# Two groups of tiny loads added to GpSimd's queue in a batched matmul-trace kernel

## The chip, the cores and the metric

The kernel runs on one core of a Trainium2 chip. The time is device time in microseconds (us) of one execution on that core. Before the change it was 707.68 us, the median of 3 runs (707.53 to 707.79).

The core has a matrix engine (TensorE, PE in the profile), a vector engine (VectorE, DVE), a scalar engine (ScalarE, ACT), a general engine (GpSimd, POOL) and a synchronizing engine (SyncE, SP). 16 DMA engines move data between the main memory (HBM) and the on-chip memory (SBUF). An engine starts a transfer by an issue on its own queue, and the transfer counts up a semaphore, by 16 in all, when it has landed.

## The reference

```python
def setup_inputs():
    B, N = 8, 2176
    return {"a": np.random.randn(B, N, N).astype(np.float32),
            "b": np.random.randn(B, N, N).astype(np.float32)}

def reference(a, b):
    prod = np.matmul(a, b)
    return np.diagonal(prod, axis1=1, axis2=2).sum(axis=-1).astype(np.float32)
```

For each of 8 batches it is the trace of A times B. The kernel never forms the product: the trace is the sum over all i and k of A[i,k] * B[k,i], so it transposes A and takes the sum of the elementwise product of A's transpose with B.

## The kernel before

A batch is two matrices of 2176 by 2176 float32 numbers, some 19 MB each, and every one of them is read once. The loads convert to bfloat16 on the way, which is why nearly all of them stand on GpSimd's queue. A matrix comes in two transfers: `middle` (5 of its 17 blocks of 128 rows) and a side tile (the other 12 blocks, as 2 groups of 6 rows for each partition). The tiles are `a_side`, `b_side`, `middle` (used by A first and then by B) and `at`, the transpose of A. There is one of each.

For a batch, PE transposes A block by block into three PSUM tiles (`fill0` to `fill2`, L301 to L311), and ACT and DVE copy these to `at` (`evacuate`, L212): of four fills, DVE takes one. Then DVE multiplies `at` by B and sums, by one instruction for the part in `middle` and one for the part in `b_side` (`rows_product`, L239, by the instruction at L234), each into a column of `sums`. A matrix product with a column of ones adds up the partitions at the end.

The order of the loads is written out by hand in GpSimd's program (L149 to L202), with waits on semaphores between them. For each batch: the middle of A (L152 or L158; from the second batch on it waits for the first product of the batch before, L157), the side of A (L162, behind a wait for the transposes of the batch before, L161), the middle of B (L176, when PE has read A's middle, L175), and the side of B (L184, when DVE has taken the second product of the batch before, L180). For the first batch a fifth of A's middle is loaded by ACT (L135) without conversion, and ACT and DVE convert it.

In the last batch the side of B comes in pieces, so that little work is left when the last byte has landed: first 6 blocks at once (L189), then three pieces by `LATE_SLICES` (L194 to L198: 3 blocks, 1 and 1), then three parts of the last block by `LAST_PIECES` (L199 to L202), each with a semaphore of its own. PE multiplies most of these (L347), DVE the rest. Small PE products that nobody reads keep PE busy between the pieces.

After its last load GpSimd counts up a semaphore 16 times (L203), drains (L207: it waits until its own work is done), waits for the last product (L208) and clears the kernel's semaphores (L209). SP stores the result (L144), and GpSimd's wait for that store (L358) ends the program.

The queue of GpSimd is in order: what is issued later is carried out later by each DMA engine. So a load that is issued early waits behind those already in the queue, and while something is queued the DMA engines have work.

Of the kernel before, what the change touches and what calls it, by code (L numbers as in the profile page):

```python
# [10 lines left out]
def kernel(  # L11
# [6 lines left out]
    nc = tc.nc  # L18
    P = 128
# [7 lines left out]
    f32 = mybir.dt.float32  # L27
# [16 lines left out]
    sb = ctx.enter_context(tc.tile_pool(name="sb", bufs=1))  # L44
# [10 lines left out]
    sums = sb.tile([P, 2 * (BATCH - 1)], f32, tag="sums")  # L55
    late_acc = sb.tile([P, NT], f32, tag="late")
    result = sb.tile([P, BATCH], f32, tag="result")

    fill_tiles = [ps.tile([P, 8, P], f32, tag=f"fill{j}", name=f"fill{j}") for j in range(BUFS)]
    trace_ps = ps.tile([P, P], f32, tag="trace")  # L60
# [2 lines left out]
    sem = {}  # L63

    own = ["first", "a_mid", "a_all", "b_mid", "b_all"]
    own += [f"piece{k}" for k in range(len(LATE_SLICES) + len(LAST_PIECES))]
    own += ["cleared", "constant", "cast", "mid_in", "all_in", "filled", "at_done", "early"]
    own += [f"free{j}" for j in range(BUFS)]
    for name in own:
        sem[name] = nc.alloc_semaphore(name)  # L70
    numbers = sorted(sem[name].num for name in own)
# [4 lines left out]
    def group(src, start, g, m):  # L76

        rows = src[start:start + P * g * m, :]
        return rows.rearrange("(g p r) k -> p g (r k)", g=g, r=m)
# [49 lines left out]
    plain = b_side.bitcast(f32).rearrange("p r k -> p (r k)")[:, :N]  # L129
    half = N // 2  # L130

    with tc.tile_critical(no_gpsimd_drain=True):

        first = a[0, 0:MID * P, :].rearrange("(p r) k -> p r k", r=MID)
        nc.scalar.dma_start(out=plain, in_=first[:, MID - 1, :]).then_inc(sem["first"], 16)  # L135
        for bi in range(BATCH):
# [8 lines left out]
            out=out.rearrange("(a b) -> a b", a=1), in_=result[:1, :BATCH],  # L145
# [3 lines left out]
        for bi in range(BATCH):  # L149
            last = bi == BATCH - 1  # L150
            if bi == 0:
                nc.gpsimd.dma_start(  # L152
                    out=middle[:, 0:MID - 1, :].rearrange("p r k -> p (r k)"),
                    in_=first[:, 0:MID - 1, :].rearrange("p r k -> p (r k)"),
                ).then_inc(sem["a_mid"], 16)
            else:
                nc.gpsimd.wait_ge(sem["product"], 2 * bi - 1)  # L157
                nc.gpsimd.dma_start(  # L158
                    out=middle.rearrange("p (g r) k -> p g (r k)", g=1), in_=group(a[bi], 0, 1, MID),
                ).then_inc(sem["a_mid"], 16)  # L160
                nc.gpsimd.wait_ge(sem["filled"], per_batch * bi)  # L161
            nc.gpsimd.dma_start(  # L162
                out=a_side.rearrange("p (g r) k -> p g (r k)", g=2),
                in_=group(a[bi], MID * P, 2, SIDE),
            ).then_inc(sem["a_all"], 16)
            if bi == 0:
                for t in (identity32, identity16):
                    nc.gpsimd.memset(t, 0.0).then_inc(sem["cleared"], 1)
                for k, t in enumerate((identity32, identity16)):
                    nc.gpsimd.wait_ge(sem["cleared"], 2)  # L170
                    nc.gpsimd.affine_select(
                        out=t, in_=t, compare_op=mybir.AluOpType.not_equal, fill=1.0, base=0,
                        pattern=[[-1, P]], channel_multiplier=1,
                    ).then_inc(sem["constant"], 1)
            nc.gpsimd.wait_ge(sem["filled"], per_batch * bi + mid_fills)  # L175
            nc.gpsimd.dma_start(  # L176
                out=middle.rearrange("p (g r) k -> p g (r k)", g=1), in_=group(b[bi], 0, 1, MID),
            ).then_inc(sem["b_mid"], 16)
            if bi:
                nc.gpsimd.wait_ge(sem["product"], 2 * bi)  # L180
            else:
                nc.gpsimd.wait_ge(sem["cast"], 2)
            if not last:
                nc.gpsimd.dma_start(  # L184
                    out=b_side.rearrange("p (g r) k -> p g (r k)", g=2),
                    in_=group(b[bi], MID * P, 2, SIDE),
                ).then_inc(sem["b_all"], 16)
                continue
            nc.gpsimd.dma_start(  # L189
                out=b_side[:, 0:SIDE, :].rearrange("p (g r) k -> p g (r k)", g=1),  # L190
                in_=group(b[bi], MID * P, 1, SIDE),
            ).then_inc(sem["b_all"], 16)
            rows = b[bi, LAST * P:N, :].rearrange("(p r) k -> p r k", r=SIDE)
            for k, (r, m) in enumerate(LATE_SLICES):  # L194
                nc.gpsimd.dma_start(  # L195
                    out=b_side[:, SIDE + r:SIDE + r + m, :].rearrange("p r k -> p (r k)"),
                    in_=rows[:, r:r + m, :].rearrange("p r k -> p (r k)"),
                ).then_inc(sem[f"piece{k}"], 16)  # L198
            for k, (lo, mid, hi) in enumerate(LAST_PIECES):  # L199
                nc.gpsimd.dma_start(  # L200
                    out=b_side[:, MOST - 1, lo:hi], in_=rows[:, SIDE - 1, lo:hi],
                ).then_inc(sem[f"piece{len(LATE_SLICES) + k}"], 16)  # L202
# [2 lines left out]
        stored = nc.gpsimd.alloc_register("stored")  # L205
        nc.gpsimd.reg_mov(stored, 16)
        nc.gpsimd.drain()  # L207
        nc.gpsimd.wait_ge(sem["product"], 2 * (BATCH - 1) + 1)  # L208
        nc.gpsimd.sem_clear(range(numbers[0], numbers[-1] + 1))  # L209

# [12 lines left out]
        for _ in range(20):  # L223
# [3 lines left out]
            out=middle[:, MID - 1, :half], in_=plain[:, :half]  # L227
# [11 lines left out]
        def rows_product(v0, rows, acc):  # L239
# [10 lines left out]
            out=middle[:, MID - 1, half:], in_=plain[:, half:]  # L250
        ).then_inc(sem["cast"], 1)
        for bi in range(BATCH):
# [12 lines left out]
            out=result[:1, 0:BATCH - 1],  # L265
            in_=total[:, 0:2 * (BATCH - 1)].rearrange("o (b n) -> o b n", n=2),
# [17 lines left out]
        for k, (lo, mid, hi) in enumerate(LAST_PIECES):  # L284
# [8 lines left out]
            out=result[:1, BATCH - 1:BATCH], in_=total[:, early:early + cols],  # L293
# [96 lines left out]
```

## Time and profile before

| | |
|---|---|
| median of 3 runs | 707.68 us (707.53 to 707.79) |
| the profiled execution | 707.76 us |
| its span, first to last instruction | 706.0 us |
| DVE busy | 380.1 us, 54% |
| PE busy | 209.0 us, 30% |
| ACT busy | 202.5 us, 29% |
| GpSimd busy | 24.5 us, 3% |
| GpSimd's DMA queue (q0) | 7392 packets, 150.96 MB written, 99.7% of the 16 engines' span |
| all DMA packets | 7544, of them 626 under 512 B |
| HBM read | 303.04 MB, 429 GB/s over the span |
| side of A or B: issue to landing, median | 54.7 us and 52.1 us |
| middle of A or B: issue to landing, median | 24.5 us and 22.0 us |

The profile counts the bytes that are written: 2 for each number loaded with conversion, where 4 are read. A transfer is cut into packets, each of them carried by one of the 16 engines. "Busy" is the time in which an engine had at least one instruction in work. The 40 slices of the page are 17.65 us each.

### The profile page before, as it was taken

The page shows a single profiled execution, that of the slowest core. Times are in us where ns is not written, and L with a number is a line of the kernel's source. Part 1 is how long each engine was busy: PE and PEld are TensorE (multiplying, and loading weights), DVE is VectorE, ACT ScalarE, POOL GpSimd, SP SyncE. Part 2 cuts the span into 40 slices and gives each one's busy share as a digit, 9 for nine tenths or more (in the row PEclk, how much of TensorE's full clock was granted, in tenths as well). Part 3 has the DMA queues.
Part 4 walks back from the last instruction along what each step waited for, and adds up shares of the span by engine and source line. Part 5 has one row for each costly group of instructions (what it writes and reads, how often), then busy time and mean ns, then how long its engine had stood idle before and what let it go on. Part 6 is the DMA issues. An engine that isn't in the chain of part 4 may idle for free. (4 is left out here: it accounts for less than half of the span.)

```text
span 706.0 us, 3981 instructions
## 1 busy us (share of the span) xinstructions
PE 209.0 (30%) x1641; PEld 190.6 (27%) x1643; DVE 380.1 (54%) x96; ACT 202.5 (29%) x158; POOL 24.5 (3%) x46
## 2 busy tenths in 40 slices
PE   0335003450134501244013440125401353012547
PEld 0335002440124401244013430124301243012535
DVE  0105488154871539716396163961639616395268
ACT  1427002370024700246003450044500455004540
POOL 1000000000000000000000000000000000002000
PEclk9859555695556955669556785556855677556778
DMA  9999999999999999999999999999999999999997
GB/s 231 219 212 209 228 211 215 216 225 213 221 220 213 206 224 216 215 213 227 209 224 221 211 210 226 214 215 219 221 207 225 222 207 214 224 217 215 225 205 156
DMA packets 7544, 152.14 MB, mean 216 GB/s; under 512 B 626, under 2 KB 882, under 8 KB 1266
## 3 DMA queue, kind: packets, MB, share of 16 engines
q0 software_dynamic: 7392, 150.96, 99.7%
q10 hardware_dynamic: 144, 1.11, 0.4%
q8 instruction: 2, 0.03, 0.0%
q14 instruction: 4, 0.03, 0.0%
q1 hardware_dynamic: 2, 0.00, 0.0%
HBM read 303.04 MB, written 0.00 MB: 429 GB/s over the span
## 5 line engine op out<-in xcount | busy, mean ns | idle before, releaser
L220 ACT COPY at<-fill 128x1536 bf16<-128x1536 bf16 (+3 forms) x156 | 200.1, 1371 | 472.1 <-DVE sums L234 356.5
L234 DVE CUSTOM_DVE_ANT_0 at<-at,b_side 128x26112 bf16<-128x26112 bf16 (+4 forms) x11 | 202.9, 18459 | 83.5 <-DMA b_side<-in_b_dram 83.5
L220 DVE COPY at<-fill 128x1536 bf16<-128x1536 bf16 (+2 forms) x52 | 83.9, 1614 | 221.2 <-PE fill L310 220.8
L310 PE MATMUL fill<-identity,middle 128*128 128x128 f32 (+1 forms) x440 | 69.9, 346 | 370.6 <-PEq L308 370.6
L310 PEld LDWEIGHTS fill<-identity,middle 128*128 128x128 f32 (+1 forms) x440 | 64.8, 182 | 375.3 <-issue 374.9
L310 PE MATMUL fill<-identity,a_side 128*128 128x128 f32 (+1 forms) x1056 | 124.6, 278 | 112.2 <-PEq L308 111.7
L310 PEld LDWEIGHTS fill<-identity,a_side 128*128 128x128 f32 (+1 forms) x1056 | 114.8, 167 | 122.2 <-issue 121.8
L234 DVE CUSTOM_DVE_ANT_0 at<-at,middle 128x10880 bf16<-128x10880 bf16 x8 | 91.9, 11490 | 11.0 <-ACTq L221 11.0
L176 POOL DMA_DIRECT2D middle<-in_b_dram x8 | 4.5, 563 | 335.2 <-PE fill L310 335.2
L158 POOL DMA_DIRECT2D middle<-in_a_dram x7 | 3.9, 563 | 292.1 <-DVE sums L234 292.1
L347 PE MATMUL trace_ps<-b_side,at 128*128 128x128 bf16 x122 | 10.0, 251 | 9.4 <-DMA b_side<-in_b_dram 9.3
L347 PEld LDWEIGHTS trace_ps<-b_side,at 128*128 128x128 bf16 x122 | 9.1, 116 | 11.3 <-DMA b_side<-in_b_dram 10.7
L162 POOL DMA_DIRECT2D a_side<-in_a_dram x8 | 5.7, 714 | 0.0
L184 POOL DMA_DIRECT2D b_side<-in_b_dram x7 | 5.0, 713 | 0.0
L347 PE MATMUL fill<-at 128*128 128x512 bf16 x19 | 4.8, 379 | 0.1
L249 DVE CAST middle<-b_side 128x1088 bf16<-128x1088 f32 x1 | 0.7, 726 | 4.9 <-DMA b_side<-in_a_dram 4.9
L347 PEld LDWEIGHTS fill<-at 128*128 128x128 bf16 x21 | 1.9, 98 | 1.5
L226 ACT ACT_TABLE_LOAD x1 | 1.3, 1283 | 2.7 <-issue 2.7
L226 ACT CAST middle<-b_side 128x1088 bf16<-128x1088 f32 x1 | 1.1, 1098 | 2.0 <-DMA b_side<-in_a_dram 2.0
L200 POOL DMA_DIRECT2D b_side<-in_b_dram x3 | 1.6, 587 | 0.0
L195 POOL DMA_DIRECT2D b_side<-in_b_dram x3 | 1.6, 558 | 0.0
L234 DVE DVE_READ_ACCUMULATOR2_ANT sums<- 128x1 f32 x14 | 1.2, 83 | 0.0
(17 smaller groups left out, 4.2 us busy)
## 6 DMA issues: line engine op xcount, KB each, us to landing
a_side<-in_a_dram POOLq DMA_DIRECT2D x8, 6528.0 KB, 54.7
b_side<-in_b_dram POOLq DMA_DIRECT2D x7, 6528.0 KB, 52.1
middle<-in_b_dram POOLq DMA_DIRECT2D x8, 2720.0 KB, 22.0
middle<-in_a_dram POOLq DMA_DIRECT2D x7, 2720.0 KB, 24.5
b_side<-in_b_dram POOLq DMA_DIRECT2D x1, 3264.0 KB, 37.5
middle<-in_a_dram POOLq DMA_DIRECT2D x1, 2176.0 KB, 14.7
b_side<-in_b_dram POOLq DMA_DIRECT2D x1, 1632.0 KB, 44.9
b_side<-in_a_dram ACTq DMA_DIRECT2D x1, 1088.0 KB, 5.1
```

The source lines that it names most:

```text
L158: nc.gpsimd.dma_start(out=middle.rearrange("p (g r) k -> p g (r k)", g=1), in_=group(a[bi], 0, 1, MID),).then_inc(sem["a_mid"], 16)
L162: nc.gpsimd.dma_start(out=a_side.rearrange("p (g r) k -> p g (r k)", g=2), in_=group(a[bi], MID * P, 2, SIDE),).then_inc(sem["a_all"], 16)
L176: nc.gpsimd.dma_start(out=middle.rearrange("p (g r) k -> p g (r k)", g=1), in_=group(b[bi], 0, 1, MID),).then_inc(sem["b_mid"], 16)
L184: nc.gpsimd.dma_start(out=b_side.rearrange("p (g r) k -> p g (r k)", g=2), in_=group(b[bi], MID * P, 2, SIDE),).then_inc(sem["b_all"], 16)
L195: nc.gpsimd.dma_start(out=b_side[:, SIDE + r:SIDE + r + m, :].rearrange("p r k -> p (r k)"), in_=rows[:, r:r + m, :].rearrange("p r k -> p ...
L200: nc.gpsimd.dma_start(out=b_side[:, MOST - 1, lo:hi], in_=rows[:, SIDE - 1, lo:hi],).then_inc(sem[f"piece{len(LATE_SLICES) + k}"], 16)
L220: copy(out=dst, in_=src).then_inc(sem[f"free{i % BUFS}"], 1)
L226: nc.scalar.copy(out=middle[:, MID - 1, :half], in_=plain[:, :half]).then_inc(sem["cast"], 1)
L234: return nc.vector.tensor_tensor_reduce(out=x if out is None else out, in0=x, in1=y, scale=1.0, scalar=0.0, op0=MUL, op1=ADD, accum_out=acc,)
L249: nc.vector.tensor_copy(out=middle[:, MID - 1, half:], in_=plain[:, half:]).then_inc(sem["cast"], 1)
L310: done = nc.tensor.transpose(into, block, identity)
L347: done = nc.tensor.matmul(trace_ps if real else fill_tiles[0][:, 0:4, :], x, y, start=(n == 0 or not real), stop=(n == len(work) - 1 or no ...
```

## The change

A tile `marks` of 2560 words on each partition is added, with a semaphore of its own. A helper `mark(base)` issues 19 loads from A's first matrix into it on GpSimd's queue, without conversion. The first 15 load 1 to 15 partitions (n partitions of base + n words each). Then a GpSimd instruction resets a cursor of the software that spreads transfers over the DMA engines (`reset_dge_cursor`). The last four load 4 partitions in 4 segments each, of base/2 + 1 to base/2 + 4 words. Nothing reads `marks`.

`mark(16)` stands behind the first batch's load of B's side (L184 of before), ahead of the wait for the first product. `mark(32)` stands in the last batch behind the first of the `LATE_SLICES` loads, ahead of the five last pieces. Behind the drain at the end, GpSimd also waits until the 38 loads have landed (38 x 16 = 608 counts), and the range of semaphores that it clears is longer by one.

```diff
+    marks = sb.tile([P, 2560], f32, tag="marks")
...
+    own += ["marks"]
...
+    marked, at_word = 0, 0
+
+    def mark(base):
+
+        nonlocal marked, at_word
+        for n in range(1, 16):
+            nc.gpsimd.dma_start(
+                out=marks[0:n, at_word:at_word + base + n], in_=a[0, 0:n, 0:base + n],
+            ).then_inc(sem["marks"], 16)
+            marked += 16
+            at_word += base + n
+        nc.gpsimd.inc_swdge_sem([], [], mode="reset_dge_cursor")
+        for n in range(1, 5):
+            nc.gpsimd.dma_start(
+                out=marks[0:4, at_word:at_word + 4 * (base + 16)].rearrange(
+                    "p (g w) -> p g w", g=4)[:, :, 0:base // 2 + n],
+                in_=a[0, 0:4, 0:256].rearrange("p (g w) -> p g w", g=4)[:, :, 0:base // 2 + n],
+            ).then_inc(sem["marks"], 16)
+            marked += 16
+            at_word += 4 * (base + 16)
...
                     in_=group(b[bi], MID * P, 2, SIDE),
                 ).then_inc(sem["b_all"], 16)
+                if bi == 0:
+                    mark(16)
                 continue
...
                 ).then_inc(sem[f"piece{k}"], 16)
+                if k == 0:
+                    mark(32)
             for k, (lo, mid, hi) in enumerate(LAST_PIECES):
...
         nc.gpsimd.drain()
+        nc.gpsimd.wait_ge(sem["marks"], marked)
         nc.gpsimd.wait_ge(sem["product"], 2 * (BATCH - 1) + 1)
```

## The prediction

> **What bounds the kernel now.** I read the slices and queues of the page first, then the chain of work that ended last, then GpSimd's timeline, then the list of DMA issues.
>
> ```profile
> DMA  9999999999999999999999999999999999999997
> GB/s 231 219 212 209 228 211 215 216 225 213 221 220 213 206 224 216 215 213 227 209 224 221 211 210 226 214 215 219 221 207 225 222 207 214 224 217 215 225 205 156
> DMA packets 7544, 152.14 MB, mean 216 GB/s; under 512 B 626, under 2 KB 882, under 8 KB 1266
> ## 3 DMA queue, kind: packets, MB, share of 16 engines
> q0 software_dynamic: 7392, 150.96, 99.7%
> ```
>
> The 16 DMA engines are busy in every slice but the last, and GpSimd's queue q0 takes 99.7% of them. Nothing else is near that: DVE, the busiest engine, has 54%. So whatever lengthens the stream of packets lengthens the kernel, wherever in the stream it stands. The end agrees:
>
> ```profile
> 649.61 0.52 POOL b_side L189
> 650.13 44.91 DMA b_side<-in_b_dram
> 695.04 0.05 issue
> ...
> 701.58 0.39 another core or an unknown queue
> ...
> 702.53 0.09 another core or an unknown queue
> 702.61 0.05 issue
> 702.66 0.65 PE trace_ps L347 x6
> ```
>
> (start, length, what). PE waits for one piece after another as it lands; from the last landing, 702.97 in the trace's semaphore records, to the end at 706.0 everything is a fixed sequence. DVE too ends on the pieces: in the timeline it idles 0.17 us for the fourth before 701.99. So the end moves with the last landing.
>
> ```profile
> 25.18 0.72 POOL L184 DMA_DIRECT2D b_side<-in_b_dram  x1
> 79.67 0.57 POOL L158 DMA_DIRECT2D middle<-in_a_dram  x1 [53.77 <-DVE sums L234]
> ...
> 649.61 0.54 POOL L189 DMA_DIRECT2D b_side<-in_b_dram  x1
> 650.13 1.61 POOL L195 DMA_DIRECT2D b_side<-in_b_dram  x3
> 651.69 1.64 POOL L200 DMA_DIRECT2D b_side<-in_b_dram  x3
> ```
>
> GpSimd issues far ahead of the engines: it idles 53.77 us behind the place of the first group, and the pieces behind the second group are issued some 45 us before they land.
>
> **The change part by part.**
>
> Issue time. 19 loads at the spacing of the last issues (1.61 us for three, some 0.52 us each) are 9.9 us per group. Group one ends near 36, long before 79.67, where GpSimd waits for the first product anyway; it would cost from 53.77/19 = 2.8 us a load. Group two moves the issue of five pieces from 650.7 to about 660.6. The first engine is done with the piece ahead near 693.4, and the longest time from an issue to a first packet in the trace is 3.6 us (1.45 to 5.05), so it costs only above (693.4 - 3.6 - 650.7)/19 = 2.1 us a load. I take nothing for both; the rows of 0.52 to 0.72 us are far below. The cursor reset is one GpSimd instruction of the kind that took 27 ns at the program's start: nothing, behind the same cover.
>
> Packets. This is the term that counts, and the packet records of the trace price it. A completion packet (4 bytes) took 22 ns and a 512 byte packet 60 ns, but they overlap. From the completion packets of the last pieces on the first engine, one piece took 2608, 1705, 651 and 349 ns, with 8 packets of 4352, 2816, 1024 and 512 bytes written. At 0.0735 ns a byte (26112 bytes took 1942 ns, 512 took 60) the bytes are 2560, 1656, 602 and 301 ns. What remains is 48 ns each time: 8 packets and one completion. A whole batch, 48 packets, four completions and 1,183,744 bytes an engine, comes round every 87.294 us, of which the bytes are 87.040: 254 ns remain. The two equations give 3.8 ns a packet and 17.6 ns a completion.
>
> For loads without a cast the ACT queue shows 8704 bytes in 328 ns, 0.0368 ns a byte. Each group has 19 completions on every engine (before: 608 packets of 4 bytes for 38 loads, 16 each). Rows and segments: 120 + 64 = 184 packets in group one; in group two 194, since the listing of instructions shows its first row cut into 11 parts of 3 words. That is 11.5 and 12.1 an engine, with 15.3 and 25.1 KB in all.
> - Group one: 19 x 17.6 + 11.5 x 3.8 + 35 = 413 ns.
> - Group two: 19 x 17.6 + 12.1 x 3.8 + 58 = 438 ns.
> - Sum 0.85 us, all on the path, as the engines never wait.
>
> Bounds: if a completion costs no more than any packet, 61.6 x 3.8 + 93 = 0.33 us. If all 48 ns of a piece were its completion's and a tiny packet cost as much as a 512 byte one in its row (41.5 ns), 38 x 48 + 23.6 x 41.5 = 2.8 us. Below nothing is excluded: no byte is taken away. I take 0.85, since two rows fix it. It lies near the lower end because a tiny load is almost all completion and completions overlap.
>
> How the packets spread matters little: at even shares an engine has 11.5. Were all loads to start on the same engine, that one would carry 15 + 16 = 31 and pay 19.5 x (3.8 + 3) = 0.13 us more a group. The trace of before has only loads of 128 partitions and cannot show it. The Trainium skill (DMA: Bandwidth & Descriptors, "Why a DMA increments its semaphore by 16 and not by 1") says that GpSimd's loads on fewer engines take consecutive ones from a round-robin cursor, and that all 16 post the completion. By it the rows of 1 to 15 fill every engine 7 or 8 times and the four segmented loads once each: the even sum, where the other reading would add 0.26 us.
>
> Drain and wait. GpSimd's drain at L207 gets 38 more loads to wait out, all landed before the last pieces; the new wait for their count follows it and is fulfilled by then. Behind it stand the clearing of semaphores and the wait for the output's landing. I take nothing, with a doubt that is the second rival.
>
> Forecast: the profiled execution took 707.76 us (its span of 706.0 and 1.76 around it) and would take 708.61; the median of the runs is 0.08 lower, 707.68, and 707.68 + 0.85 = **708.5**, its own range 708.0 to 709.0. That is 0.12% more, and 0.2% (1.4 us) is about what a measurement of this kernel can tell from no change.
>
> **The rivals.**
>
> 1. *Tiny packets cost more than the two equations say* (709.1 to 710.5). No row has a data packet under 512 bytes in this queue, and if a read's latency is not covered for some 31 tiny packets in a row, the price goes to the upper bound. For it: nothing in before tests it. Against: the 512 byte packets lost nothing beyond their bytes.
>
> 2. *The drain walks its list* (slower). In the instruction records L207's drain ends at 704.56, 1.59 us after the last landing, far more than a drain without loads behind it (34 to 187 ns). If that is a walk over 38 loads, it is 42 ns each, and 76 loads make it 3.18 us. GpSimd's wait for the output ended at 705.18 and it was ready for it near 704.84, so 0.33 us are covered; from 8 added loads on the drain decides the end. Price 1.59 - 0.33 = 1.26 us, time 709.8. Against: loads that landed long before could have been ticked off while it waited.
>
> 3. *Each tiny load holds its engine until it has landed.* The last completion packet ended at 702.70 and counted at 702.97: 0.27 us, times 38 is 10.3 us, 718. Against: the last three pieces landed at 701.97, 702.61 and 702.97 with 48 ns beyond their bytes. The Trainium skill (same page, "Anatomy of one DMA — SWDGE (gpsimd) path") speaks against the change more strongly: about 2.0 us fixed per DMA, mostly completion. Paid 38 times in a row that would be an estimated 76 us; by those landings the trace does not agree that it is paid in a row.
>
> 4. *Nothing is seen* (707.4 to 708.0): the last engine's final completion counts 0.26 us behind the next one's and 1.45 behind the first one's, and that engine might be spared most of the packets. 5. *Faster*: only if the uneven engines were evened out; no row gives a way.
>
> **How the numbers follow.** Forecast 0.40; tiny packets dearer 0.18 (0.02 of it still within 0.2%); drain 0.28; engine held, or issue beyond its cover, 0.06; nothing 0.05; faster 0.03. Within 0.2%: 0.40 + 0.02 + 0.05 = 0.47. Slower: 0.16 + 0.28 + 0.06 = 0.50. Faster: 0.03. The forecast is the likeliest single case, though the slower ones together hold slightly more. The range 708.0 to 710.6 takes in the forecast, both ends of the packet price and the drain on top of it, and leaves out 0.14.
>
> **What would show it.** Packets rise from 7544 by 38 x 16 + 184 + 194 = 986 to about 8530, nearly all under 512 B; fewer mean that not all engines post completions. The issues of `marks` last near 0.5 us each; the wait before the next batch's middle load shrinks from 53.77 by some 10 us and its start stays near 79.7. The last landing moves from 702.97 to about 703.8 and the drain still ends 1.6 us behind it; near 3.2 it is rival 2. Landings later than 704.4 mean rival 1, and issues above 2 us each would make the forecast wrong from GpSimd's side.

## The result, and the profile after

The changed kernel takes 713.31 us (median of 3 runs, 712.88 to 713.52) against 707.68 us: 5.63 us more, ratio 1.0079 with a 95% interval of 1.0056 to 1.0102. It is slower, by less than one per cent but clear of the noise, and by more than the range allowed for. The profiled execution took 713.31 us, its span is 711.2 us.

Queue and packets, from the page of the changed kernel:

```profile
GB/s 234 213 215 221 213 183 230 210 215 226 208 216 220 215 216 222 211 220 219 212 225 213 216 221 210 227 213 214 223 208 224 220 205 226 210 217 226 211 213 118
DMA packets 8760, 152.19 MB, mean 214 GB/s; under 512 B 1842, under 2 KB 2098, under 8 KB 2482
q0 software_dynamic: 8608, 151.01, 99.7%
```

The queue is as full as before by its share of time, but the sixth slice (88.9 to 106.7 us) moved 183 GB/s where before it was 211. That is where group one stands, behind the first batch's side of B. 1216 packets came on top, not 986. By their sizes they are 608 completions, 250 rows, 32 segmented partitions (one packet each, the segments joined) and 326 fillers of 4 or 16 bytes. That is 32 packets for each load, so by these counts an engine without a share in a load carries a filler, and each load put two packets on every engine.

A closer look at that place: three stretches of the kernel before, and then the same three of the changed kernel (busy time of the engines, clock, and as the last two columns the DMA engines' share and GB/s):

```profile
89.00:91.00 2.00, 0.00 (x0) 0.00 (x0) 0.00 (x0) 0.00 (x0) 0.00 (x0) 0.50 0.83 176
91.00:95.00 4.00, 0.00 (x0) 0.00 (x0) 3.55 (x1) 0.00 (x0) 0.00 (x0) 0.50 1.09 234
95.00:105.00 10.00, 0.41 (x2) 0.44 (x3) 10.00 (x1) 0.00 (x0) 0.00 (x0) 0.50 1.04 223
```

```profile
89.00:91.00 2.00, 0.00 (x0) 0.00 (x0) 0.00 (x0) 0.00 (x0) 0.00 (x0) 0.50 1.83 185
91.00:95.00 4.00, 0.00 (x0) 0.00 (x0) 3.39 (x1) 0.00 (x0) 0.00 (x0) 0.50 0.46 93
95.00:105.00 10.00, 0.00 (x0) 0.00 (x0) 10.00 (x1) 0.00 (x0) 0.00 (x0) 0.50 1.03 222
```

A packet's time is put down where it starts, so a share can be over 1. In the changed kernel 15 engines have started a packet of the next load by 90.8 and the last one by 91.6, and none starts another before 93.5: 1.83 and then 0.46. The packet records show why: 16 packets of 21,760 bytes just behind the group took 3.26 to 3.67 us, where the median is 1.62. The list of DMA issues shows what they stood behind (KB, and us from issue to landing):

```profile
marks<-in_a_dram POOLq DMA_DIRECT2D x1, 0.1 KB, 65.0
marks<-in_a_dram POOLq DMA_DIRECT2D x1, 0.1 KB, 64.7
marks<-in_a_dram POOLq DMA_DIRECT2D x1, 0.2 KB, 64.4
marks<-in_a_dram POOLq DMA_DIRECT2D x1, 0.3 KB, 64.1
```

They were issued some 0.5 us apart and each stayed 0.3 us less in the queue than the one ahead, so they landed some 0.2 us apart, 19 of them in about 4 us, though the packets of one engine start and end within some 0.3 us.

GpSimd's side is as forecast:

```profile
25.78 7.43 POOL L140 DMA_DIRECT2D marks<-in_a_dram  x15
33.20 2.39 POOL L147 DMA_DIRECT2D marks<-in_a_dram  x4
79.01 0.57 POOL L181 DMA_DIRECT2D middle<-in_a_dram  x1 [43.42 <-DVE sums L262]
...
654.32 7.41 POOL L140 DMA_DIRECT2D marks<-in_a_dram  x15
661.72 2.38 POOL L147 DMA_DIRECT2D marks<-in_a_dram  x4
```

0.5 us a load, the wait 10.35 us shorter and ended no later. The end of the chain (start, length, what):

```profile
665.72 40.75 DMA b_side<-in_b_dram
...
706.52 0.65 PE trace_ps L375 x6
...
707.78 0.15 DVE result L320
```

The last piece lands at 706.82, 3.86 us later than before. The end moved by 5.23 us, from 705.99 to 711.22, so 1.37 us more were lost behind the last landing. There GpSimd's drain ends at 709.98, 3.16 us after the landing; it was 1.60 us. The drain before, and then that of the changed kernel (its length in ns, given three times as there is only one, and its start):

```profile
L207 POOLq DRAIN  x1: 50866/50866/50866, 653.7 to 653.7; - x1
```

```profile
L234 POOLq DRAIN  x1: 43876/43876/43876, 666.1 to 666.1; - x1
```

Two costs, then: 1.93 us for each group in the stream, and 1.4 us at the end.

### The profile page after: what moved, and what is told of

Read it like the earlier page. It is cut to its first block, busy times and chain, and to the rows that moved or that the text cites. A ratio compares the mean times of both kernels' runs of the same rounds, so it can differ in the third digit from the quotient of the medians.

```text
span 711.2 us, 4022 instructions
## 1 busy us (share of the span) xinstructions
PE 208.6 (29%) x1641; PEld 189.4 (27%) x1643; DVE 380.3 (53%) x96; ACT 202.3 (28%) x158; POOL 44.0 (6%) x84
## 5 line engine op out<-in xcount | busy, mean ns | idle before, releaser
L140 POOL DMA_DIRECT2D marks<-in_a_dram x30 | 14.8, 506 | 0.0
L207 POOL DMA_DIRECT2D b_side<-in_b_dram x7 | 4.9, 706 | 0.0
L147 POOL DMA_DIRECT2D marks<-in_a_dram x8 | 4.8, 601 | 0.0
L220 POOL DMA_DIRECT2D b_side<-in_b_dram x3 | 1.7, 568 | 0.0
```

Source lines behind the costliest of these rows:

```text
L140: nc.gpsimd.dma_start(out=marks[0:n, at_word:at_word + base + n], in_=a[0, 0:n, 0:base + n],).then_inc(sem["marks"], 16)
L147: nc.gpsimd.dma_start(out=marks[0:4, at_word:at_word + 4 * (base + 16)].rearrange("p (g w) -> p g w", g=4)[:, :, 0:base // 2 + n], in_=a[0 ...
L207: nc.gpsimd.dma_start(out=b_side.rearrange("p (g r) k -> p g (r k)", g=2), in_=group(b[bi], MID * P, 2, SIDE),).then_inc(sem["b_all"], 16)
L220: nc.gpsimd.dma_start(out=b_side[:, SIDE + r:SIDE + r + m, :].rearrange("p r k -> p (r k)"), in_=rows[:, r:r + m, :].rearrange("p r k -> p ...
```

## The experiments

I first put the four microseconds down to the counting: 16 engines with 19 completions each are 304 counts, 13 ns apart. Theory S holds one semaphore for the narrow place, theory C the way that all counts take, theory P the tiny packets themselves. For the drain, theory W says that it takes 42 ns for each load in its list, behind the last landing. The ratios are to runs of the kernel before that were taken beside the experiments, with a median of 707.83 us.

**e1_own_sems**: 19 semaphores instead of one, for all 38 loads. GpSimd waits for them ahead of its drain instead of behind it.

```diff
-            ).then_inc(sem["marks"], 16)
+            ).then_inc(sem[f"marks{marked // 16 % 19}"], 16)
```

> The 19 loads of a group count on 19 semaphores of their own instead of one. Theory S (one semaphore takes the counts of all engines one after the other, 304 in 4.0 us, and the engines cannot write on until theirs are taken): no pile-up, each group costs its packets alone, about 0.4 us, the last landing near 703.8; with the longer drain (76 loads, 1.35 us more at the end) some 709.9 us. Theory C (it is the way that all counts take, whatever the semaphore) and theory P (each tiny packet costs some 50 ns in its engine): nothing changes, 713.3 us, each group 1.9 us.

712.83 us, ratio 1.0069 (1.0052 to 1.0086). The last landing is 0.48 us sooner than in the change, no more. Theory S falls as the cause: one semaphore is about an eighth of the 3.86 us.

This run also settles more than it was made for, since each load now has its own counts. The trace does not name the engine of a count; I take the first count of each load for the earliest engine and the last for the latest. In group one the earliest engine counted its first load at 90.328 and its 19th at 93.662, 0.185 us a load; the latest came 1.32 us after it, at 91.649, and counted its 19th at 94.612, 0.165 us a load. Between 94.288 and 94.612, when most engines were done, only some five counts were taken, and the latest engine still needed 0.16 us for each. A common way that takes a count in 13 ns was free then. So theory C falls too: **each engine by itself needs 0.17 to 0.2 us from one completion to the next**, and 13 ns is about that divided by 16. One thing stays open: in the change no two counts on the one semaphore are closer than 11 ns, 0.19 us for 16 of them, while here counts come as close as 2 ns. So the one semaphore may have held the engines just above their own pace, which could be the 0.48 us; whether it or its recording sets the 11 ns is not shown. The later runs were read with this theory, O; for their numbers it says the same as C did.

**e2_few_loads**: about the same number of packets, few completions. Each group is 4 loads of 128 partitions; the segmented loads and the cursor reset are left out.

```diff
-        for n in range(1, 16):
+        for n in range(1, 5):
...
-                out=marks[0:n, at_word:at_word + base + n], in_=a[0, 0:n, 0:base + n],
+                out=marks[:, at_word:at_word + base + n], in_=a[0, 0:P, 0:base + n],
...
```

> Each group is 4 loads of 128 partitions and 17 to 20 or 33 to 36 words: 36 packets an engine, as many as the 38 of the change, but 4 counts an engine instead of 19. Theories S and C (64 counts, 0.85 us, which what was read ahead covers): 0.3 us a group at most, a drain over 46 loads (1.93 us, 0.33 of the 0.34 more being covered), 708.0 to 708.4 us. Theory P (51 ns a packet): 1.8 us a group, 711.4 us.

708.34 us, ratio 1.0007 (0.9997 to 1.0016): not to be told from before. From the landing of B's side to that of the next middle 12.96 us pass, 12.85 before, and 14.77 in the change. Theory P falls: 36 packets an engine with 4 completions cost a tenth of a microsecond there, 38 with 19 cost 1.92. The last landing is 0.32 us later in all.

**e3_spread**: the same 38 loads, at most five in a row.

```diff
-                    mark(16)
+                for k in range(5 * bi, 5 * bi + 5):
+                    tiny(k)
...
-                    mark(32)
+                    for t in range(35, 38):
+                        tiny(t)
```

> The same 38 loads on the same semaphore, five behind each of the first seven batches' side of B and three behind the first late piece. Theories S and C with a pile-up that the engines cover up to about 2.1 us (80 counts take 1.06 us): only the packets' own time, 0.85 us in all, and the drain's 1.35: 709.9 us. Theory P, or a loss in proportion to the counts: 3.9 + 1.35, 712.9 us.

709.55 us, ratio 1.0024 (1.0014 to 1.0034). The stream lost 0.36 us in all instead of 3.86. The first two of those stretches have no hole in this kernel:

```profile
89.00:91.00 2.00, 0.00 (x0) 0.00 (x0) 0.00 (x0) 0.00 (x0) 0.00 (x0) 0.50 0.88 177
91.00:95.00 4.00, 0.00 (x0) 0.00 (x0) 3.60 (x1) 0.00 (x0) 0.00 (x0) 0.50 0.99 212
```

What remains is the drain, 3.15 us behind the last landing.

**e5_double** and **e6_half**: how the loss grows with the number in a row.

```diff
# e5_double
-                    mark(16)
+                    mark(2), mark(2)
...
-                    mark(32)
+                    mark(2), mark(2)
# e6_half
-        for n in range(1, 16):
+        for n in range(1, 16, 2):
...
-        for n in range(1, 5):
+        for n in range(1, 3):
```

> Two times 19 loads at each of the two places (narrower ones, base 2, so that they fit), all on the one semaphore. With a pile-up that is covered up to 2.1 us (608 counts, 8.0 us): 5.9 us a group, 11.8 in all. With a loss in proportion to the loads: 3.9 us a group, 7.7 in all. Drain theory W (42 ns for each of the loads of the whole program): 114 loads, 4.8 us behind the last landing, 2.8 more than before at the end. So 722.3 us or 718.2 us.

> 10 of the 19 loads at each place (odd numbers of partitions, two segmented ones). With a pile-up that is covered up to 2.1 us (160 counts, 2.1 us): only the packets' 0.2 us a group; in proportion: 1.0 us a group. Drain theory W: 58 loads, 2.4 us behind the last landing, 0.5 more at the end. So 708.6 us or 710.2 us.

722.91 us, ratio 1.0212 (1.0195 to 1.0229), and 708.86 us, ratio 1.0015 (1.0005 to 1.0024). Both are near what a cover of some 2 us forecast, and far from a loss in proportion to the loads. Group one cost 5.70 us with 38 loads and 0.13 us with 10; it was 1.92 with 19, and 0.09 with the five of e3_spread. From 19 to 38 that is 0.20 us a load, and the line meets zero between 9 and 10 loads. So about 1.9 us of completions in a row are covered, and beyond them each load costs what a completion needs. e6_half keeps the cursor reset, which e2_few_loads, e3_spread and e9_sync_queue leave out, so the reset is not what costs. The sixth slice of the double one is deeper, 154 GB/s where the change has 183:

```profile
GB/s 232 209 213 221 209 154 213 217 221 220 214 220 214 220 209 224 210 223 210 223 212 225 213 222 214 220 210 224 209 220 214 222 211 226 209 224 213 222 171 90
```

**e7_first_only**: group one alone.

```diff
-                if k == 0:
-                    mark(32)
```

> The group in the last batch is left out. The first alone costs 1.93 us at the last landing (704.9). Drain theory W (42 ns for each load since the start): 57 loads, 2.4 us behind the last landing, 0.46 more at the end: 710.1 us. Drain theory W2 (only loads that have not landed when the drain begins, 28 of them in the change against 9): 1.6 us as before, 709.6 us.

710.44 us, ratio 1.0035 (1.0022 to 1.0047). The last landing is 1.96 us later than before, the drain's end is 2.38 us behind it. These loads had landed some 560 us before the drain began, and it still took 0.78 us more. Theory W2, by which only loads that have not landed yet count, falls.

**e8_drain_between**: one more drain, in the batch before the last.

```diff
+                if bi == BATCH - 2:
+                    nc.gpsimd.drain()
                 continue
```

> The change with one more drain of GpSimd, behind the side of B of the batch before the last. That drain has to wait for a landing that comes some 12 us after the next issue is due, so the queue runs dry for 2 to 4 us. Drain theory W, if a drain strikes its loads off the list: the last drain has 29 loads left and ends 1.2 us behind the last landing instead of 3.2, the end gains 1.35: about 715 us. If the list is never struck off: 3.2 us as in the change, about 716.5 us.

718.27 us in one run. The new drain waited until 619.06, 1.97 us past the landing of B's side at 617.09 with 47 loads in its list, and the queue ran dry:

```profile
564.30 0.70 POOL L207 DMA_DIRECT2D b_side<-in_b_dram  x1
619.57 0.56 POOL L181 DMA_DIRECT2D middle<-in_a_dram  x1 [54.56 <-issue]
```

The issue came 14.2 us later than in the change, and the last landing 6.3 us later, more than I had allowed. But the last drain then had 29 loads and ended 1.23 us behind the last landing: a drain strikes its loads off the list.

**e9_sync_queue**: the same loads on SP's hardware queue.

```diff
-            nc.gpsimd.dma_start(
+            nc.sync.dma_start(
...
+            if bi == 0:
+                mark(16)
+            if bi == BATCH - 1:
+                mark(32)
```

> The same 38 loads on SP's hardware queue, the first group when A's side of the first batch has landed, the second when that of the last batch has; the cursor reset is left out. SP issues one in some 0.3 us, so that counts cannot pile up, and GpSimd's drain has 38 loads as before. Theories S and C: 0 to 0.5 us in all, 707.7 to 708.2 us. Theory P: some 140 packets of 51 ns over 16 engines, 0.5 us a group, 708.7 us. A drain that is long for another reason than its list of loads would add 1.35 to either.

707.89 us, ratio 1.0000 (0.9990 to 1.0010): the 38 loads cost nothing that can be measured. The drain is 1.60 us, as before. Nearly all of these packets stood alone between two large ones (nine in ten took the 22 to 28 ns of a packet that follows one with a cast); the last load of group one landed only at 134.46, 81 us after its issue, for SP's queue and GpSimd's took turns packet by packet.

What the end gains without GpSimd's drain was not tried.

The drain in all kernels, from the instruction records and the landings:

| kernel | loads in the list | us from last landing to drain's end | ns a load |
|---|---|---|---|
| e8_drain_between, last drain | 29 | 1.23 | 42 |
| before; e9_sync_queue | 38 | 1.60; 1.60 | 42 |
| e2_few_loads | 46 | 1.93 | 42 |
| e8_drain_between, first drain | 47 | 1.97 | 42 |
| e7_first_only | 57 | 2.38 | 42 |
| e6_half | 58 | 2.42 | 42 |
| the change; e1_own_sems; e3_spread | 76 | 3.16; 3.16; 3.15 | 42 |
| e5_double | 114 | 4.71 | 41 |

Theory W holds at eight lengths of the list; the time behind the last landing goes by the number of loads. What the drain does in that time the traces do not show.

## Why the prediction was wrong, point by point

**What bounds the kernel**: right. The stream of packets never pauses for lack of work, and a loss at 90 us arrives whole at the end: 1.96 us in e7_first_only.

**Issue time**: right, 0.50 us a load and 0.6 for the segmented ones, all covered.

**Packets: the step that failed.** "The two equations give 3.8 ns a packet and 17.6 ns a completion", and from this 0.85 us; measured 3.86. The equations are sound for where they come from: on the late pieces a completion comes after 8 packets, of which even the shortest have 0.30 us of bytes. By this reading a completion's own 0.17 to 0.2 us passes behind that, and only 17.6 ns stick out. In the change 19 completions follow each other on an engine, started only some 12 to 26 ns apart, so the hidden time becomes the pace. The upper bound failed for the same reason: it took the 48 ns that stick out for all that a completion can cost. The lesson is in the row: a price that was measured behind a cover says nothing of the price without it. Two kinds of term were needed, time on the engine (38 small packets, some 0.3 us of packet records where 0.41 and 0.44 were forecast, near enough) and time in a chain of completions.

Rival 1, dearer tiny packets, is not what happened, although its sign, a landing later than 704.4, came: e2_few_loads has nearly as many tiny packets and loses a tenth of a microsecond where the change loses 1.92. Rival 3 was nearest in kind, a load that holds its engine until it has landed, 0.27 us each. But I let it hold from the first load on, and got 10.3 us and a chance of 0.06 shared with another; with 0.2 us and the cover of 1.9 us a group, both known only from the runs, it gives 2 x (19 x 0.2 - 1.9) = 3.8 us.

Why a completion takes that long was not tried by itself. The Trainium skill (DMA: Bandwidth & Descriptors, "Queues, rings and completion order") describes the completion as a strongly ordered write, which lands only after every earlier write of its engine; 0.165 us a load on an engine that was nearly the last one counting would fit a wait of that kind. The same page ("Anatomy of one DMA — SWDGE (gpsimd) path") calls the bubble of that write about one cycle. The trace does not bear out that completions in a row come that cheap; whether the time is in the write or in the wait ahead of it, no run here tells. What covers the first 1.9 us also stays open. It is the same before packets of 21,760 bytes and of 4,352 (group one 1.92, group two 1.88 us), so it is not the length of the one packet behind.

**The spread over the engines**: right that it hardly matters, for another reason: with its filler every engine carries two packets for every load.

**Drain and wait: the second step that failed.** "I take nothing, with a doubt that is the second rival." The rival was right to the number: 3.18 us forecast from 42 ns a load, 3.16 measured; price 1.26 us, measured 1.37, of which some 0.07 is the new wait for the loads' count that follows the drain. What I held against it, that early loads could be ticked off while the drain waits, is refuted by e7_first_only. The row was there: for the 1.59 us behind the last landing I had no other explanation.

**The sum**: 3.86 + 1.37 = 5.23 us, which is the span's growth. The profiled execution grew by 5.55 us; the other 0.3 us lie outside the span, and the profile does not show where. The range ended at 710.6: it held the packet term's upper bound (2.8 us) or the drain's price, not both. Both together give 711.7, still short, since the upper bound was too low.

## What to carry to other kernels

Many small loads behind each other on GpSimd's queue are paid by the load, not by the byte, once more than some nine completions stand in a row: put a few behind each large transfer, join them into one, or give them to a hardware queue where they stand between large packets. Count the loads that GpSimd has issued since its last drain: 42 ns for each stand behind the last landing, and they are free only as long as something else ends later. When a price is read from a row, ask what passed beside it in that row.

## What the runs showed that I had not expected

- By the counts of packets, a load of fewer than 16 partitions on GpSimd's queue puts a filler packet on each engine without a share: 326 for 38 loads.
- 4 segments of one partition were joined into one packet on GpSimd's queue (32 packets for 8 loads). On SP's queue they were packets of their own, of 36 to 48 bytes in group one.
- SP's queue counted 155 times for group one: 136 for the engines that carried data, and 19, one for each load, for the rest of its 16.
- A tiny packet takes 9 to 20 ns when it follows another without a cast, and 22 to 28 ns when it follows one with a cast.
